# A transformer block on one core: order of VectorE's rows around the norms, short sums in last rows, and the first tiles of the second FFN in turn

## The chip, the cores and the metric

The kernel runs on one core of a Trainium2 chip. The metric is the device time of one execution in microseconds (us). The kernel before takes 1902.46 us, the median of three runs (1902.03 to 1902.89).

## The reference

One encoder block for 256 tokens of width 2048: a half-step SwiGLU FFN (inner width 5632), a mixing stage of 16 attention heads of width 128, and a second FFN. Shift, scale and gate of each come from one vector c.

```python
def rms_norm(x, g):
    y = xf * lax.rsqrt(jnp.mean(xf * xf, axis=-1, keepdims=True) + EPS)
    return (y * g.astype(jnp.float32)).astype(x.dtype)
...
mod = jax.nn.silu(c) @ w_ada[l] + b_ada[l]
sh1, sc1, gt1, sh2, sc2, gt2, sh3, sc3, gt3 = jnp.split(mod, N_MOD, axis=-1)
f = swiglu(modulate(rms_norm(h, g_ffn1[l]), sh1, sc1), w1_gate[l], w1_up[l], w1_down[l])
h = h + 0.5 * gt1[:, None, :] * f
nrm = modulate(rms_norm(h, g_mix[l]), sh2, sc2)
qkv = nrm @ w_qkv[l]
...
qa = rms_norm(q[:, :, :N_HEADS_NA], qn_na[l])
qb = partial_rope(rms_norm(q[:, :, N_HEADS_NA:], qn_dil[l]), cos, sin)
...
o_na = rms_norm(o_na.reshape(B, S, D_NA), g_out_na[l])
o_dil = rms_norm(o_dil.reshape(B, S, D_DIL), g_out_dil[l])
mix = jnp.concatenate([o_na, o_dil], axis=-1) @ w_o[l]
h = h + gt2[:, None, :] * mix
f = swiglu(modulate(rms_norm(h, g_ffn2[l]), sh3, sc3), w2_gate[l], w2_up[l], w2_down[l])
h = h + 0.5 * gt3[:, None, :] * f
```

Heads 0 to 7 attend to a neighbourhood on a grid, heads 8 to 15 to dilated windows; both kinds are computed here as full 256 x 256 scores with a bias added (-1e30 where nothing is seen).

## The kernel before

**Layout.** Activations are held transposed: h is 16 tiles of 128 features by 256 tokens, and nx holds the normed h, each tile as a rounded half (hi) beside its remainder (low). Weights come as 644 chunks of 128 x 1024, in one list (srcs) in the order of use: w1_s, a, b, d, c, e for the first FFN, w_qkv (96 chunks), w_o (32), then w2_a, b, d, c, e.

**One chunk.** SP loads it (wraw, L159, five buffers), ScalarE casts it to hi (L167), VectorE subtracts to get the remainder low (L168); hi and low have four buffers each. W.chunk asks for a chunk three ahead of the one that TensorE multiplies (AHEAD = 3). In the same place rows of w_ada are issued at a paced rate, and VectorE reduces them to the modulation vectors (L147). After a chunk that is issued with a w_ada row, that row's load is kept behind it in SP's queue.

**Products.** mm2 multiplies hi by both halves of the activation at once (512 columns, L173) and low by the first half (256 columns, L174) into a bank of 512 columns, whose two halves have to be added afterwards: by two L401 in the FFN's down product, by an ACT copy and L643 in the output projection. mm3 makes three products of 256 or 512 columns into one sum (L179), with nothing to add afterwards.

**Stages.** In the FFN the gate and up products of a tile of 128 inner features use the first k's of the model width first (up_first: 6 in the first FFN, K2 = 8 in the second), for tile after tile, then the rest; down products follow in two parts (ffn_down), whose last row d = 15 is followed by the row statistic (Stat.add) and a norm. Stat.add squares each h tile on ScalarE, or the last one on VectorE (L222), adds them up in sqa (L232), and TensorE sums over the partitions by a product with ones (pstat, L235 for sqa, L236 for the last square). rstd_from makes the reciprocal root: Ln and Exp on ScalarE (L199 is the Ln), and one Newton step on VectorE (L205, L207 to L209). norm_mod forms h times gain times root (nt, L244), adds the shift while rounding (ACT L247) and takes the remainder (L248). Around a norm TensorE runs idle matmuls (pw, L190).

**The mixing stage** is a list of units, one weight chunk each. For each of four groups of heads 8 units make v, 8 make k and 8 make q. Steps that follow are put in slots: at(u, fn) runs fn behind unit u. For k and q these are the squares (u + 1), the root over 8 values a row (u + 2, rqr) and the scaling with rope (qk_norm, u + 3, L590 to L605). The heads of a group follow 24 units later by PLAN (PLAN_L for the last group, whose heads run beside the first 16 units of the output projection): transposes of k and q (pT, L673), scores, softmax, transposes of p, and p times v. The last scores product comes with d_ew, which also adds the statistic over eight heads (ost). The projection has 32 units: b = 0 (heads 0 to 7), then b = 1, with 16 rows d each; fin scales a product (L644) by gate and root and adds it to h (L645).

**What sets the order.** TensorE's order is that of the program text (MANUAL). The order on the other engines is decided by the scheduler before the run, by priorities: a step's place in the text less an offset where it stands in tc.high_priority (URGENT = 400, SOON = 60). SP issues the loads in the order so decided, and each load waits for a free buffer.

Of the kernel before, what the change touches and what calls it, by code (L numbers as in the profile page):

```python
# [15 lines left out]
P = 128  # L16
# [35 lines left out]
PLACE = ((44, 40),) + 7 * ((48, 0),)  # L52
MANUAL = {mybir.EngineType.PE}
# [12 lines left out]
def build(tc, a):  # L66
    nc = tc.nc
    with ExitStack() as ctx:
# [47 lines left out]

        queue = []
# [93 lines left out]

        class Stat:
# [5 lines left out]
            def add(self, t, last_dve=True):  # L218
                sq = sp.tile([P, S], F32, tag="sq", name="sq")
                self.n += 1  # L220
                if self.n == self.total and last_dve:
                    nc.vector.tensor_tensor(sq, t, t, ALU.mult)  # L222
                else:
                    nc.scalar.activation(sq, t, AF.Square)
# [16 lines left out]
        def norm_mod(k, r, jsh, jsc, full=None):  # L241
            sh, gs = mods[jsh], mods[jsc]
            t = sp.tile([P, S], F32, tag="nt", name="nt")
            nc.vector.scalar_tensor_tensor(t, h[k], gs[:, k : k + 1], r, ALU.mult, ALU.mult)  # L244
            if full is not None:
                nc.scalar.activation(full, t, AF.Identity, bias=sh[:, k : k + 1])
            nc.scalar.activation(nx[k][:, 0, :], t, AF.Identity, bias=sh[:, k : k + 1])  # L247
# [53 lines left out]
        class W:  # L301
            def __init__(self):
# [5 lines left out]
                self.credit = 0.0  # L308

# [17 lines left out]
            def chunk(self, ahead=AHEAD):  # L327
                while self.head <= min(self.tail + ahead, len(srcs) - 1):
                    self.ready[self.head] = wsplit(wraw(srcs[self.head][0]), srcs[self.head][1])
# [9 lines left out]
                return self.ready.pop(self.tail - 1)  # L339

# [14 lines left out]
        def up_first(f, part, kx):  # L355
            ps = pair("pa")
            up_mm(ps, 0, kx, True, True)
            part[f] = hp.tile([P, 2, S], F32, tag="hid", name=f"pt{f}")
# [28 lines left out]
        def ffn_down(fs, hid, gate, stat=None, out=None):  # L387
            acc_ = {}
            for d, f in down_order(fs):
                if d not in acc_:  # L390
                    acc_[d] = bank("pd")
                mm2(acc_[d], *ws.next(), hid[f], f == fs[0], f == fs[-1])
# [4 lines left out]
                if d == KT - 1 and stat is not None:  # L397
                    idle(9)
                with tc.high_priority(offset=URGENT if stat is not None and d >= KT - 2 else 0):
                    for part_ in (ps[:, :S], ps[:, S:]):  # L400
                        nc.vector.scalar_tensor_tensor(h[d], part_, g, h[d], ALU.mult, ALU.add)  # L401
                    if stat is not None:
                        stat.add(h[d])
                if out is not None:
# [137 lines left out]
        with tc.tile_pool(name="att", bufs=2) as ap_, tc.tile_pool(name="atc", bufs=1) as ac:  # L542
# [71 lines left out]
            def qkv_unit(u, g, j, nm, cch, st_):  # L614
                def go(whi, wlo):
# [10 lines left out]
                    if cch == 7:  # L626
# [3 lines left out]
                        else:  # L630
                            at(u + 1, lambda: qk_squares(nm, ps, st_))
                            at(u + 2, lambda: qk_rstd(st_))
                            for t in range(2):
                                at(u + 3 + t // QS, lambda t=t: qk_norm(g, j, nm, ps, t, st_))
                return go

            def wo_unit(u, b, d):
                def fin(ps):
# [3 lines left out]
                    nc.scalar.copy(t, ps[:, :S])  # L642
                    nc.vector.tensor_tensor(t, t, ps[:, S:], ALU.add)  # L643
                    nc.vector.scalar_tensor_tensor(t, t, mods[5][:, d : d + 1], rows[b], ALU.mult, ALU.mult)  # L644
# [4 lines left out]
                def last_fin(ps):  # L649
                    if d == KT - 1:  # L650
                        idle(9)
                    with tc.high_priority(offset=URGENT):
                        fin(ps)

                def go(whi, wlo):
                    ps = bank("pso")
                    for kk in range(8):
                        sl = slice(kk * P, (kk + 1) * P)
                        mm2(ps, whi[:, sl], wlo[:, sl], ox[b * 8 + kk], kk == 0, kk == 7)
# [3 lines left out]
            def head(g, i, a0, b0, c0, d0):  # L663
                hd = g * 4 + i
                s_ = {}
# [9 lines left out]
                def a_ew():  # L675
                    with tc.high_priority(offset=SOON):
# [11 lines left out]
                def b_ew1():  # L688
                    with tc.high_priority(offset=SOON):
# [10 lines left out]
                def b_ew2():  # L700
                    with tc.high_priority(offset=SOON):
# [15 lines left out]
                def c_ew():  # L717
                    with tc.high_priority(offset=SOON):
# [11 lines left out]
                def d_ew():  # L730
                    po = s_["po"]
                    go = vec[:, GO + hd : GO + hd + 1]
                    nc.scalar.activation(ox[hd][:, 0, :], po, AF.Copy, scale=go)
                    nc.vector.scalar_tensor_tensor(
                        ox[hd][:, 1, :], po, go, ox[hd][:, 0, :].bitcast(F32), ALU.mult, ALU.subtract)
                    ost[hd // 8].add(po, False)
# [169 lines left out]
```

## Time and profile before

| | |
|---|---|
| median of three runs | 1902.46 us |
| the profiled execution, its own time | 1902.98 us |
| its span, first to last instruction | 1901.2 us |
| mean granted TensorE clock | 0.996 of full speed |
| data read from HBM | 500.09 MB, 264 GB/s over the span |
| last down product of the first FFN, start | 762.09 us |

The page gives busy times of engines: PE is TensorE's matmuls, PEld its weight loads, DVE VectorE, ACT ScalarE, POOL GpSimd, SP SyncE. A group's row reads out<-in, the tile's size, the count (x2), and in brackets how long the engine had been idle before it and what ended that: [3.02 <-DVE qn L605] is 3.02 us of idleness ended by VectorE's write of qn in line 605. A timeline row begins with the start in us and the time that its instructions took, those of a row together.

### The profile page before, as it was taken

What the parts mean: (1) busy time and instruction counts of PE and PEld (TensorE: products, weight loads), DVE (VectorE), ACT (ScalarE), POOL (GpSimd) and SP (SyncE); (2) the same over time, 40 slices, a digit from 0 to 9 for tenths busy, and PEclk for the clock granted to TensorE, in tenths of its full rate; (3) what the DMA queues carried; (4) which work ended last, traced back from release to release, by engine and by line L of the source; (5) the groups of instructions that cost most, each with busy time, mean ns of one, the idle gap of its engine ahead of it and who ended that gap; (6) DMA issues with size and microseconds to landing.
All of it is one profiled execution on the core that took longest, in us unless ns stands there. A gap on an engine that the chain in (4) does not pass through costs nothing.

```text
span 1901.2 us, 27533 instructions
## 1 busy us (share of the span) xinstructions
PE 1873.3 (99%) x10564; PEld 1633.8 (86%) x10564; DVE 1563.3 (82%) x2123; ACT 907.4 (48%) x1333; POOL 0.7 (0%) x6
## 2 busy tenths in 40 slices
PE   8999999999999999999999999999999999999999
PEld 6877888888888888888888888888888888888888
DVE  7899999988888889878887898888799986556565
ACT  2444545443334454555555565544555543334442
POOL 0000000000000000000000000000000000000000
PEclk9999999999999999999999999999999999999999
DMA  9988888889998987777765544888677876666664
GB/s 393 397 327 299 307 301 303 303 314 337 334 328 324 334 309 247 257 260 248 263 234 174 153 154 157 320 294 303 212 276 262 279 269 220 191 194 193 191 206 135
DMA packets 120227, 503.98 MB, mean 265 GB/s; under 512 B 13344, under 2 KB 15904, under 8 KB 101664
## 3 DMA queue, kind: packets, MB, share of 16 engines
q1 hardware_dynamic: 120096, 502.24, 75.9%
q8 instruction: 82, 1.34, 0.3%
q14 instruction: 49, 0.40, 0.1%
HBM read 500.09 MB, written 2.10 MB: 264 GB/s over the span
## 4 chain that ended last, share of the span: by engine, by line
PE 89%; DVE 6%; DMA 2%; ACT 1%; issue 1%; SPq 0%; ACTq 0%; DVEq 0%
PE pb L173 23%; PE pd L173 17%; PE pb L174 11%; PE pa L173 9%; PE pd L174 8%; PE pqk L179 5%; PE pqq L179 5%; PE pa L174 4%; PE pqv L179 4%; DVE low L168 2%; DMA rx<-in_w_ada_dram 2%; PE pso L173 1%; DVE rx L147 1%; DVE ra L147 1%; PE pso L174 1%
## 5 line engine op out<-in xcount | busy, mean ns | idle before, releaser
L167 ACT CAST hiw<-rw 128x1024 fp32r<-128x1024 f32 x644 | 674.6, 1050 | 713.1 <-PE pd L173 238.5
L168 DVE TENSOR_TENSOR low<-rw,hiw 128x1024 fp32r<-128x1024 f32 x644 | 785.9, 1222 | 264.3 <-ACT hiw L167 262.9
L173 PE MATMUL pb<-nx,hiw 128*128 128x512 f32 x1920 | 654.8, 389 | 0.0
L174 PE MATMUL pb<-nx,low 128*128 128x256 f32 x1920 | 530.8, 277 | 1.2 <-DVE low L168 1.2
L173 PE MATMUL pd<-hd,hiw 128*128 128x512 f32 x1408 | 480.1, 389 | 0.0
L173 PEld LDWEIGHTS pb<-nx,hiw 128*128 128x128 f32 x1920 | 360.3, 188 | 75.7
L174 PE MATMUL pd<-hd,low 128*128 128x256 f32 x1408 | 389.1, 276 | 0.0
L174 PEld LDWEIGHTS pb<-nx,low 128*128 128x128 f32 x1920 | 360.4, 188 | 1.9 <-DVE low L168 1.8
L173 PEld LDWEIGHTS pd<-hd,hiw 128*128 128x128 f32 x1408 | 264.3, 188 | 55.5
L173 PE MATMUL pa<-nx,hiw 128*128 128x512 f32 x800 | 275.1, 391 | 1.7 <-ACT hiw L167 1.2
L174 PEld LDWEIGHTS pd<-hd,low 128*128 128x128 f32 x1408 | 264.3, 188 | 0.0
L147 DVE CUSTOM_DVE_ANT_0 ra<-ra,cb,vec 128x2048 f32<-128x2048 f32 x101 | 237.0, 2346 | 3.3 <-DMA ra<-in_w_ada_dram 3.3
L174 PE MATMUL pa<-nx,low 128*128 128x256 f32 x800 | 220.9, 278 | 4.3 <-DVE low L168 4.3
L173 PEld LDWEIGHTS pa<-nx,hiw 128*128 128x128 f32 x800 | 149.5, 188 | 34.6 <-ACT hiw L167 2.4
L174 PEld LDWEIGHTS pa<-nx,low 128*128 128x128 f32 x800 | 150.2, 188 | 7.8 <-DVE low L168 6.8
L147 DVE CUSTOM_DVE_ANT_0 rx<-rx,cb,vec 128x2048 f32<-128x2048 f32 x43 | 100.9, 2347 | 1.5 <-DMA rx<-in_w_ada_dram 1.5
L173 PE MATMUL pso<-ox,hiw 128*128 128x512 f32 x256 | 90.4, 398 | 0.0
L179 PE MATMUL pqk<-hiw,nx 128*128 128x512 f32 x256 | 84.3, 395 | 0.0
L179 PE MATMUL pqq<-hiw,nx 128*128 128x512 f32 x256 | 83.0, 393 | 0.0
L179 PE MATMUL pqv<-hiw,nx 128*128 128x512 f32 x256 | 81.4, 392 | 0.3 <-ACT nx L247 0.3
L401 DVE SCALAR_TENSOR_TENSOR h<-pd,m,h 128x256 f32<-128x256 f32 x128 | 60.8, 482 | 20.0 <-PE pd L174 17.8
L174 PE MATMUL pso<-ox,low 128*128 128x256 f32 x256 | 71.6, 280 | 0.0
(138 smaller groups left out, 1510.0 us busy)
## 6 DMA issues: line engine op xcount, KB each, us to landing
ra<-in_w_ada_dram SPq DMA_DIRECT2D x101, 1024.0 KB, 7.2
rw<-in_w_b_dram SPq DMA_DIRECT2D x144, 512.0 KB, 4.5
rw<-in_w_d_dram SPq DMA_DIRECT2D x128, 512.0 KB, 4.2
rw<-in_w_a_dram SPq DMA_DIRECT2D x100, 512.0 KB, 5.2
rw<-in_w_c_dram SPq DMA_DIRECT2D x96, 512.0 KB, 4.1
rw<-in_w_qkv_dram SPq DMA_DIRECT2D x96, 512.0 KB, 4.1
rx<-in_w_ada_dram SPq DMA_DIRECT2D x43, 1024.0 KB, 7.3
rw<-in_w_e_dram SPq DMA_DIRECT2D x48, 512.0 KB, 4.5
```

The costliest lines, as they stand in the source:

```text
L147: ins = nc.vector.tensor_tensor_reduce(out=raw, in0=raw, in1=cb, scale=1.0, scalar=vec[:, BA + i : BA + i + 1], op0=ALU.mult, op1=ALU.add, ...
L167: casts[:] = casts[-1:] + [nc.scalar.copy(hi, raw)]
L168: lows[:] = lows[-1:] + [nc.vector.tensor_tensor(lo, raw, hi.bitcast(F32), ALU.subtract)]
L173: nc.tensor.matmul(out, lh, r, start=first, stop=False)
L174: nc.tensor.matmul(out[:, :S], ll, r[:, 0, :], start=False, stop=last)
L179: nc.tensor.matmul(out, l, r, start=first and i == 0, stop=last and i == 2, **kw)
L401: nc.vector.scalar_tensor_tensor(h[d], part_, g, h[d], ALU.mult, ALU.add)
```

## The change

It has six parts.

1. **rstd_first** takes the place of rstd for the two norms over h (r2 ahead of the mixing stage, r3 ahead of the second FFN). The square of the root goes to ScalarE, and the first nt is formed from the unfinished root and scaled by the Newton factor itself; norm_mod takes it as t.
2. **Late splits.** While TensorE is at the last chunk ahead of w_qkv or w2_a, the newly asked-for chunk is loaded, but its cast and remainder are put behind the statistic's last square (split_late). The chunk after it is loaded and split after the norm of k = 1 (more).
3. **Short sums.** The last row (d = 15) of both FFNs' second down part, and the last SLIM = 4 rows of the projection's b = 1, use mm3 instead of mm2: 12, 32 and 12 triples in place of pairs.
4. **Idle matmuls** ahead of a statistic: 9 become 3 (first FFN) and 5 (projection).
5. **Precedence in the mixing stage.** Squares, roots and scalings of all q and k go into high_priority SOON, URGENT for the last q. The heads of the last group get URGENT instead of SOON; d_ew gets a priority, and the statistic over eight heads (d_st) goes one unit later.
6. **up_heads** begins the second FFN: for the first KA = 3 k's four tiles take turns, then each goes on alone; w2_a is laid out to match.

```diff
+        def rstd_first(ps, n, k, jsc):
...
+            nc.scalar.activation(t0, ps, AF.Ln, scale=1.0 / n, bias=epst)
+            nc.vector.tensor_scalar(t1, ps, -0.5 / n, -0.5 * EPS, ALU.mult, ALU.add)
+            nc.scalar.activation(r, t0, AF.Exp, scale=-0.5)
+            nc.scalar.activation(t0, r, AF.Square)
+            nc.vector.scalar_tensor_tensor(t, h[k], mods[jsc][:, k : k + 1], r, ALU.mult, ALU.mult)
+            nc.vector.tensor_tensor(t0, t0, t1, ALU.mult)
+            nc.vector.scalar_tensor_tensor(t, t0, 1.5, t, ALU.add, ALU.mult)
+            nc.vector.scalar_tensor_tensor(r, t0, 1.5, r, ALU.add, ALU.mult)
+            return r, t
...
             def chunk(self, ahead=AHEAD):
+                if self.tail in (first["w_qkv"] - 1, first["w2_a"] - 1):
+                    self.late = []
                 while self.head <= min(self.tail + ahead, len(srcs) - 1):
-                    self.ready[self.head] = wsplit(wraw(srcs[self.head][0]), srcs[self.head][1])
+                    raw = wraw(srcs[self.head][0])
+                    if self.late is None:
+                        self.ready[self.head] = wsplit(raw, srcs[self.head][1])
+                    else:
+                        self.late.append((self.head, raw))
...
+            def split_late(self, ins):
+                for c, raw in self.late:
+                    self.ready[c] = wsplit(raw, srcs[c][1])
+                    after(lows[-1], ins, "late")
+                self.late = None
+
+            def more(self, ins):
+                while self.head <= self.tail + AHEAD:
+                    self.ready[self.head] = wsplit(wraw(srcs[self.head][0]), srcs[self.head][1])
+                    self.head += 1
+                    after(casts[-1], marks["act"], "late")
+                    after(lows[-1], ins, "late")
...
+        def up_heads(fs, part, kx):
+            ps = {f: pair("pa") for f in fs}
+            for k in range(KA):
+                for f in fs:
+                    for j in range(2):
+                        mm2(ps[f][:, j, :], *ws.next(), nx[k], k == 0, False)
+            for f in fs:
+                up_mm(ps[f], KA, kx, False, True)
+                park2(ps[f], f, part)
...
-                mm2(acc_[d], *ws.next(), hid[f], f == fs[0], f == fs[-1])
+                slim = d == KT - 1 and (stat is not None or out is not None)
+                if slim:
+                    wh, wl = ws.next()
+                    mm3(acc_[d][:, :S], wh, wl, hid[f][:, 0, :], hid[f][:, 1, :], f == fs[0], f == fs[-1])
+                else:
+                    mm2(acc_[d], *ws.next(), hid[f], f == fs[0], f == fs[-1])
...
-                    idle(9)
+                    idle(3)
...
-                    for part_ in (ps[:, :S], ps[:, S:]):
+                    for part_ in (ps[:, :S],) if slim else (ps[:, :S], ps[:, S:]):
...
-            r2 = st.rstd(D)
+            r2, t = rstd_first(st.ps, D, 0, 4)
             for k in range(KT):
-                last = norm_mod(k, r2, 3, 4)
+                last = norm_mod(k, r2, 3, 4, t=t if k == 0 else None)
+                if k == 1:
+                    ws.more(last)
...
+                            def soon(fn, *args):
+                                with tc.high_priority(offset=URGENT if g == 3 and j == 0 else SOON):
+                                    fn(*args)
+
+                            at(u + 1, lambda: soon(qk_squares, nm, ps, st_))
+                            at(u + 2, lambda: soon(qk_rstd, st_))
...
             def wo_unit(u, b, d):
+                slim = b == 1 and d >= KT - SLIM
...
-                        idle(9)
+                        idle(5)
                     with tc.high_priority(offset=URGENT):
                         fin(ps)
+                        if d == KT - 1:
+                            ws.split_late(hst.sq)
...
+                rank = URGENT if g == 3 else SOON
...
-                    ost[hd // 8].add(po, False)
+                def d_st():
+                    with tc.high_priority(offset=rank):
+                        ost[hd // 8].add(s_["po"], False)
...
-        for f in range(F1):
+        up_heads(range(NF1), part, K2)
+        for f in range(NF1, F1):
             up_first(f, part, K2)
```

The order of instructions follows from these priorities, so it is shown at three places, all on VectorE. The first is the end of the first FFN, from the last h to the second norm step. Before:

```order
L401 SCALAR_TENSOR_TENSOR h_82<-pd,m_90,h_82 128x256 x2
L168 TENSOR_TENSOR low<-rw,hiw 128x1024
L222 TENSOR_TENSOR sq<-h_82 128x256
L205 TENSOR_SCALAR rs_7027<-pstat 128x256
L207 TENSOR_TENSOR rs_7026<-rsr 128x256
L208 TENSOR_TENSOR rs_7026<-rs_7026,rs_7027 128x256
L209 SCALAR_TENSOR_TENSOR rsr<-rs_7026,rsr 128x256
L244 SCALAR_TENSOR_TENSOR nt<-h_79,m_92,rsr 128x256 x2
L248 SCALAR_TENSOR_TENSOR nx_97<-nt,m_91,nx_97 128x256
```

And with the change (line numbers are those of the changed file):

```order
L458 SCALAR_TENSOR_TENSOR h_82<-pd,m_90,h_82 128x256
L240 TENSOR_TENSOR sq<-h_82 128x256
L171 TENSOR_TENSOR low<-rw,hiw 128x1024
L221 TENSOR_SCALAR rs_7032<-pstat 128x256
L224 SCALAR_TENSOR_TENSOR nt<-h_79,m_92,rsr 128x256
L225 TENSOR_TENSOR rs_7031<-rs_7031,rs_7032 128x256
L226 SCALAR_TENSOR_TENSOR nt<-rs_7031,nt 128x256
L227 SCALAR_TENSOR_TENSOR rsr<-rs_7031,rsr 128x256
L263 SCALAR_TENSOR_TENSOR nt<-h_79,m_92,rsr 128x256
L267 SCALAR_TENSOR_TENSOR nx_97<-nt,m_91,nx_97 128x256
```

One h step is gone, the remainder stands behind the square, and nx_97 (the first nx) has the root's last step and the second nt ahead of it.

The second place is the last q norm (qn_10001 and qn_10007 are the same tile, the second half of the tokens), where the first units of the projection run. Before:

```order
L643 TENSOR_TENSOR wt<-wt,pso 128x256
L598 TENSOR_TENSOR ra<-qn_9962,rope 128x128
L599 TENSOR_TENSOR rb<-qn_9962,rope 128x4x16
L602 TENSOR_TENSOR rb<-qn_9962,rope 128x4x16
L644 SCALAR_TENSOR_TENSOR wt<-wt,m_93,rsr 128x256
L605 TENSOR_TENSOR qn_9962<-ra,rb 128x4x32
L645 TENSOR_TENSOR h_79<-h_79,wt 128x256
L168 TENSOR_TENSOR low<-rw,hiw 128x1024
L590 SCALAR_TENSOR_TENSOR qn_10001<-pqq_9589,rqr,gq_8601 128x128 x4
L643 TENSOR_TENSOR wt<-wt,pso 128x256
```

With the change:

```order
L651 SCALAR_TENSOR_TENSOR qn_10007<-pqq_9595,rqr,gq_8607 128x128
L666 TENSOR_TENSOR qn_9968<-ra,rb 128x4x32
L651 SCALAR_TENSOR_TENSOR qn_10007<-pqq_9595,rqr,gq_8607 128x128 x2
L211 TENSOR_TENSOR rs_9931<-rs_9931,rs_9932 128x256
L659 TENSOR_TENSOR ra<-qn_10007,rope 128x128
L660 TENSOR_TENSOR rb<-qn_10007,rope 128x4x16
L663 TENSOR_TENSOR rb<-qn_10007,rope 128x4x16
L212 SCALAR_TENSOR_TENSOR rsr<-rs_9931,rsr 128x256
L666 TENSOR_TENSOR qn_10007<-ra,rb 128x4x32
L714 TENSOR_TENSOR wt<-wt,pso 128x256 x2
L715 SCALAR_TENSOR_TENSOR wt<-wt,m_93,rsr 128x256 x2
L716 TENSOR_TENSOR h_79<-h_79,wt 128x256 x2
```

The projection's steps (wt, h) and the remainder that stood between the two halves of the norm now follow both.

The third place is the end of the projection, the last rows of h up to the statistic's last square. Before:

```order
L643 TENSOR_TENSOR wt_11037<-wt_11037,pso_10989 128x256
L232 TENSOR_TENSOR sqa_10640<-sqa_10640,sq_11011 128x256
L644 SCALAR_TENSOR_TENSOR wt_11037<-wt_11037,m5_93,rsr_10596 128x256
L645 TENSOR_TENSOR h3_82<-h3_82,wt_11037 128x256
L168 TENSOR_TENSOR low_11139<-rw_11136,hiw_11138 128x1024
L232 TENSOR_TENSOR sqa_10640<-sqa_10640,sq_11042 128x256
L643 TENSOR_TENSOR wt_11055<-wt_11055,pso_11020 128x256
L644 SCALAR_TENSOR_TENSOR wt_11055<-wt_11055,m5_93,rsr_10596 128x256
L645 TENSOR_TENSOR h3_82<-h3_82,wt_11055 128x256
L222 TENSOR_TENSOR sq_11060<-h3_82 128x256
```

With the change:

```order
L710 SCALAR_TENSOR_TENSOR wt_11034<-pso_10972,m5_93,rsr_10602 128x256
L710 SCALAR_TENSOR_TENSOR wt_11067<-pso_11009,m5_93,rsr_10602 128x256
L716 TENSOR_TENSOR h3_82<-h3_82,wt_11034 128x256
L716 TENSOR_TENSOR h3_82<-h3_82,wt_11067 128x256
L250 TENSOR_TENSOR sqa_10646<-sqa_10646,sq_11000 128x256
L250 TENSOR_TENSOR sqa_10646<-sqa_10646,sq_11037 128x256
L250 TENSOR_TENSOR sqa_10646<-sqa_10646,sq_11070 128x256
L710 SCALAR_TENSOR_TENSOR wt_11079<-pso_11042,m5_93,rsr_10602 128x256
L716 TENSOR_TENSOR h3_82<-h3_82,wt_11079 128x256
L240 TENSOR_TENSOR sq_11082<-h3_82 128x256
L171 TENSOR_TENSOR low_11088<-rw_11040,hiw_11087 128x1024
```

Ahead of the square neither L643 nor a remainder is left; the remainder stands behind it. On TensorE, pstat of the second eight heads moves behind the eight products of the first unit of b = 1.

More of the change, by code (lines that the diff above doesn't have):

```diff
@@ L52 @@
 PLACE = ((44, 40),) + 7 * ((48, 0),)
+KA = 3
+SLIM = 4
 MANUAL = {mybir.EngineType.PE}
@@ L115, in build @@
         hold = []
+        marks = {}
         queue = []
@@ L210, in rstd_from @@
             return r
+        def rstd_first(ps, n, k, jsc):
+            t0 = sp.tile([P, S], F32, tag="sq", name="rs0")
+            t1 = sp.tile([P, S], F32, tag="nt", name="rs1")
+            t = sp.tile([P, S], F32, tag="nt", name="nt")
+            r = sp.tile([P, S], F32, tag="rsr", bufs=2, name="rsr")
+            nc.scalar.activation(t0, ps, AF.Ln, scale=1.0 / n, bias=epst)
[7 more added lines that the diff above has]
+            return r, t
         class Stat:
@@ L339, in chunk @@
                 return self.ready.pop(self.tail - 1)
+            def split_late(self, ins):
+                for c, raw in self.late:
+                    self.ready[c] = wsplit(raw, srcs[c][1])
+                    after(lows[-1], ins, "late")
+                self.late = None
+            def more(self, ins):
[4 more added lines that the diff above has]
+                    after(lows[-1], ins, "late")
             def next(self):
@@ L688, in b_ew1 @@
                 def b_ew1():
-                    with tc.high_priority(offset=SOON):
+                    with tc.high_priority(offset=rank):
                         sc = ap_.tile([P, 2, S], F32, tag="sc", name="sc")
@@ L700, in b_ew2 @@
                 def b_ew2():
-                    with tc.high_priority(offset=SOON):
+                    with tc.high_priority(offset=rank):
                         sc, sm = s_["p"], s_["sm"]
@@ L717, in c_ew @@
                 def c_ew():
-                    with tc.high_priority(offset=SOON):
+                    with tc.high_priority(offset=rank):
                         s_["ph"] = ap_.tile([P, 2, S], F32R, tag="ph", name="ph")
@@ L774, in build @@
             with tc.high_priority(offset=URGENT):
-                r3 = hst.rstd(D)
+                r3, t = rstd_first(hst.ps, D, 0, 7)
                 for k in range(K2):
-                    last = norm_mod(k, r3, 6, 7)
+                    last = norm_mod(k, r3, 6, 7, t=t if k == 0 else None)
+                    if k == 1:
+                        ws.more(last)
             hold.append(last)
@@ L873, in flat @@
             return x.reshape(-1, P, P)
-        arr[f"w{l}_a"] = stream(gu[NF0 if l == 1 else 0 : F1, :, :kx])
+        if l == 1:
+            arr["w1_a"] = stream(gu[NF0:F1, :, :kx])
+        else:
+            arr["w2_a"] = stream(np.concatenate([
+                flat(gu[:NF1, :, :KA].transpose(2, 0, 1, 3, 4)), flat(gu[:NF1, :, KA:kx]),
+                flat(gu[NF1:F1, :, :kx])]))
         arr[f"w{l}_b"] = stream(np.concatenate([
```

50 lines of the change are left out of this document (31 added, 19 removed).

## Prediction

> **What bounds the kernel now.** I read the shares and the chain of waits first, then TensorE's waits, then the stretches round them.
>
> ```profile
> PE 1873.3 (99%) x10564; PEld 1633.8 (86%) x10564; DVE 1563.3 (82%) x2123; ACT 907.4 (48%) x1333; POOL 0.7 (0%) x6
> PE 89%; DVE 6%; DMA 2%; ACT 1%; issue 1%; SPq 0%; ACTq 0%; DVEq 0%
> PE pT L673 <- DVE qn L605: 3.3, 2, 3.0
> PE pstat L235 <- DVE sqa L232: 3.1, 2, 1.7
> PE pstat L236 <- DVE sq L222: 1.0, 1, 1.0
> PE pa L494 <- ACT xf L246: 4.7, 2, 4.3
> ```
>
> TensorE is the bound, and the change takes no matmul of the layer away. What it can win is time in which TensorE waits, fills with idle matmuls (pw) or runs at a low clock. A row of waits gives the total, the count and the longest. L673, L235 and L236 are waits in or at the end of the mix stage, which the change touches; L494 is the kernel's start, which it does not touch. The idle matmuls count as busy, so the two norms have to be read from the timeline (start, length).
>
> **The end of the first FFN.**
>
> ```profile
> 762.40 1.00 DVE L401 SCALAR_TENSOR_TENSOR h<-pd,m,h 128x256 f32<-128x256 f32 x2
> 763.37 1.23 DVE L168 TENSOR_TENSOR low<-rw,hiw 128x1024 fp32r<-128x1024 f32 x1
> 764.51 0.42 DVE L222 TENSOR_TENSOR sq<-h 128x256 f32<-128x256 f32 x1
> 764.98 0.70 PE L236 MATMUL pstat<-sq,ones 128*128 128x256 f32 x2
> 765.30 3.31 PEld L190 LDWEIGHTS pw<-ident,ones 128*128 128x128 f32 x28
> 765.72 0.47 ACT L199 ACTIVATE rs<-pstat,epst 128x256 f32<-128x256 f32 x1 [2.38 <-PE pstat L236]
> 766.67 0.43 DVE L207 TENSOR_TENSOR rs<-rsr 128x256 f32<-128x256 f32 x1
> 768.05 0.88 DVE L244 SCALAR_TENSOR_TENSOR nt<-h,m,rsr 128x256 f32<-128x256 f32 x2
> 769.13 0.50 PE L179 MATMUL pqv<-hiw,nx 128*128 128x512 f32 x1 [0.33 <-ACT nx L247]
> ```
>
> Before the square stand two L401 and one remainder (low). The short sum leaves one L401 (half of 1.00, so 0.5), and the remainder goes behind the square: 764.51 - 763.37 = 1.14. From the reciprocal root to nt there are three VectorE steps of 0.46 ((768.05 - 766.67) / 3) and nt itself. Now ScalarE squares while VectorE forms h times gain times root, then one product, then the scaling: one step of 0.46 less. Together 0.5 + 1.14 + 0.46 = 2.1. Two things hold some back. The 14 idle matmuls behind the second pstat end at 768.6 (765.30 + 3.31), so an earlier nx 0 would have to wait for them unless they move up with the square. And the low half of nx 0 stands behind the root's own last step and the next nt (two steps of 0.46; before, one). I take **-1.75**, between 1.2 and 2.1. The remainder put off runs while VectorE waits for pstat, 1.3 us before L207 here, so it is hidden; if the square came later it would cost up to 1.14. The next chunk's split goes into the norms, but TensorE needs that chunk only after three others at 2.7 us each. The loads that step with it on SP (a chunk before the w_ada row) have over 8 us too. Fewer idle matmuls cost nothing where TensorE would wait for the square anyway.
>
> **The last q norm.**
>
> ```profile
> 1069.53 0.16 DVE L209 SCALAR_TENSOR_TENSOR rqr<-rq,rqr 128x8 f32<-128x8 f32 x1
> 1074.87 0.27 PE L673 MATMUL pT<-ident,qn 128*128 128x128 f32 x1
> 1075.59 1.11 DVE L590 SCALAR_TENSOR_TENSOR qn<-pqq,rqr,gq 128x128 f32<-128x128 f32 x4
> 1077.82 0.28 DVE L605 TENSOR_TENSOR qn<-ra,rb 128x128 f32<-128x128 f32 x1
> 1078.16 0.40 PE L673 MATMUL pT<-ident,qn 128*128 128x128 f32 x1 [3.02 <-DVE qn L605]
> 1074.00:1078.00 4.00, 1.14 (x9) 0.82 (x7) 4.00 (x13) 1.32 (x2) 0.00 (x0) 1.00 0.25 79
> 1078.00:1082.00 4.00, 3.84 (x14) 3.31 (x15) 4.00 (x8) 0.86 (x2) 0.00 (x0) 0.57 0.44 142
> 1118.00:1124.00 6.00, 4.26 (x25) 3.63 (x25) 6.00 (x14) 3.35 (x7) 0.00 (x0) 1.00 0.33 117
> 1168.00:1172.00 4.00, 2.08 (x6) 1.53 (x7) 2.43 (x6) 0.15 (x1) 0.00 (x0) 0.80 1.02 418
> 800.00:1060.00 260.00, 259.68 (x1255) 217.18 (x1254) 208.37 (x344) 140.95 (x311) 0.00 (x0) 1.00 0.70 234
> 1060.00:1170.00 110.00, 103.50 (x624) 91.73 (x622) 101.85 (x209) 65.39 (x136) 0.00 (x0) 0.98 0.53 166
> ```
>
> The stretches give their length, then busy time of TensorE, its loads, VectorE, ScalarE and POOL, and after these the granted clock. From rqr to the last qn pass 8.6 us, of which the norm's own rows are 8 scalings of 0.27 and two ropes of some 0.7 (1077.82 + 0.28 - 1076.7, the end of the scalings, less one wt step of 0.4), together 3.6. The rest is output-projection steps and a remainder. In the new order only three steps of the row norm (0.33 each) stay between: 1069.53 + 3.6 + 1.0 = 1074.1, ahead of the transpose at 1074.87. The wait of 3.02 goes, and with it the slow clock behind it: (1 - 0.57) x 4 = 1.7. The wait of 1.7 at L235 near 1120 (the longest of its row) goes too, since pstat of the second eight heads moves behind the next output unit's 2.7 us. That is 6.4.
>
> Something is late next: VectorE. It was busy 101.85 of 110 us here. Less two remainders (2.3) and four L643 (1.6) it has 97.9 left, so this stretch cannot shrink by more than 12. Adding up its new rows by these durations, the remainders for the second unit behind the transpose and for the tenth output unit arrive 0.3 and 1.1 us after TensorE asks. I take **-5.0** (6.4 - 1.4), with 0 (all given back to remainders) and 6.4 as ends.
>
> **The end of the mix stage.**
>
> ```profile
> 1156.21 1.22 DVE L168 TENSOR_TENSOR low<-rw,hiw 128x1024 fp32r<-128x1024 f32 x1
> 1157.35 0.42 DVE L232 TENSOR_TENSOR sqa<-sqa,sq 128x256 f32<-128x256 f32 x1
> 1157.68 0.41 DVE L643 TENSOR_TENSOR wt<-wt,pso 128x256 f32<-128x256 f32 x1
> 1158.13 0.48 DVE L644 SCALAR_TENSOR_TENSOR wt<-wt,m,rsr 128x256 f32<-128x256 f32 x1
> 1158.65 0.43 DVE L645 TENSOR_TENSOR h<-h,wt 128x256 f32<-128x256 f32 x1
> 1158.99 1.22 DVE L168 TENSOR_TENSOR low<-rw,hiw 128x1024 fp32r<-128x1024 f32 x1
> 1165.29 0.28 PE L174 MATMUL pso<-ox,low 128*128 128x256 f32 x1
> 1170.59 1.22 PE L236 MATMUL pstat<-sq,ones 128*128 128x256 f32 x2 [1.01 <-DVE sq L222]
> 1171.85 0.47 ACT L199 ACTIVATE rs<-pstat,epst 128x256 f32<-128x256 f32 x1 [4.04 <-PE pstat L236]
> 1175.88 0.47 PE L173 MATMUL pa<-nx,hiw 128*128 128x512 f32 x1
> 1182.75 0.39 PE L173 MATMUL pa<-nx,hiw 128*128 128x512 f32 x1
> ```
>
> A unit of the projection costs VectorE 1158.99 - 1156.21 = 2.78, a little over TensorE's 2.72, so it ends late: the last product is done at 1165.40 (1165.29 and 0.11 for 256 columns), and pstat has its square 5.2 us later. The new order puts another row between the steps that depend on each other, where a step costs 0.33 as sqa does here instead of 0.45 and 0.52, so a unit falls to about 2.5; the four short units lose L643, and two remainders (1.14 each) go behind the square. VectorE then catches up, and what is left behind the last product is scaling, adding, square (0.52 + 0.45 + 0.45, and 0.2 for the start), 1.6 us at best; I take 2.2, so **-3.0** (0.5 to 3.6). Then from pstat to the first matmul of the second FFN: 5.3 us now, of which 0.5 comes from the slow clock (Ln starts 1.26 after pstat, 1171.85 - 1170.59; at the first norm 0.74, 765.72 - 764.98). With that and the step of 0.46, less the later low half, 4.5: **-0.8**. Then the second FFN's first 16 pairs of matmuls took 6.87 us (1182.75 - 1175.88) at 0.34 a pair, 5.44 at TensorE's own pace: one tile has only four matmul pairs for each two norms. With four tiles in turn a k has 8 pairs, 2.72 us, and norms with their remainders run ahead: **-1.3**.
>
> **The tail and the short sums.**
>
> ```profile
> 854.35 0.71 PE psc L179 x6
> 1897.05 0.23 PE pd L173
> 1897.43 1.00 DVE L401 SCALAR_TENSOR_TENSOR h<-pd,m,h 128x256 f32<-128x256 f32 x2 [3.07 <-PE pd L174]
> ```
>
> At the very end one of two L401 goes (half of 1.00): **-0.5**. The short sum is three matmuls of 256 columns, 0.71 / 2 = 0.355 for a triple, where a pair costs 0.34 (0.23 for its 512 columns, half as much for 256): 56 triples (12 + 32 + 12) by 0.015 are **+0.8**. The other, small wait of L673 goes with the earlier norms: **-0.3**. The rest of the precedence moves rows inside stretches in which TensorE does not wait; I cost it at nothing, as remainders are three chunks (8 us) ahead, and a norm with rope holds VectorE for about 5.
>
> **Sum**: 1.75 + 5.0 + 3.0 + 0.8 + 1.3 + 0.5 + 0.3 - 0.8 = 11.9 us, from the profiled execution's 1902.98 (a span of 1901.2), which lies 0.5 above the median of 1902.46. So **1890.6** against the median.
>
> **Rivals.**
> VectorE becomes the bound of the projection: the 5.0 is given back as waits for remainders. For it: 101.85 busy of 110. Against: interleaved steps are shorter. 1902.5 - 6.9 = 1895.6. Chance 0.17.
>
> The clock: with 9 idle matmuls cut to 3 and 5, TensorE could be slow at both norms. At a granted clock of 0.80, as at 1168, 3.31 us of idle matmuls would take 0.8 more (3.31 / 0.8 - 3.31), and Ln came 0.5 later there: 1.3 a norm, 2.6 in all, 1893.2. Against: the wait of 1.7 left the clock at 1.00 (1118 to 1124), and the gaps I expect are below that. Chance 0.07. [...]
>
> Slower: norms put ahead of remainders in the projections of q, k and v. From the point where VectorE falls over 6 us behind, TensorE waits for a remainder, and a wait of 3 us costs 3.02 + 1.7 = 4.7 as at 1078. Four of the seven norms moved make 19: about 1909. Against: from 800 to 1060 VectorE is busy 208.37 of 260 us, 80%, and TensorE is idle for 0.3. Chance 0.04.
>
> The change does not do what it says: an order decided beforehand, with VectorE as late as before, 1901. Chance 0.04.
>
> **Chances.** The forecast has 0.68. Its own range, from the ends of its terms, is 1887 to 1894; the first rival and the clock stretch it to 1896.5. A measurement of this kernel tells about 0.2% (3.8 us) from no change. Faster by more: 0.68 + 0.17 + 0.07, 0.92. Within: 0.05. Slower: 0.03.
>
> **What would show it.** Right: no wait of pT for qn; granted clock 1.0 at 1075 to 1090; pstat's square 2 to 3 us after the last product; no gaps in the first 16 pairs of the second FFN; one L401 at the end. Wrong: waits of pso, pqv or pqk for low; a granted clock below 0.9 behind either norm; the first matmul of the mix stage later than 5 us after the first FFN's last.

## The result, and the profile after

The changed kernel takes 1889.65 us (six runs, 1889.38 to 1891.08) against 1902.5 for the kernel before on the same chip: a ratio of 0.9934, with a 95% interval from 0.9922 to 0.9947. That is 12.85 us less. The profiled execution took 1889.59, with a span of 1887.8; before, 1902.98 and 1901.2.

The page of the kernel after, busy times and the chain that ended last:

```profile
PE 1866.0 (99%) x10600; PEld 1630.3 (86%) x10600; DVE 1556.9 (82%) x2117; ACT 905.4 (48%) x1331; POOL 0.7 (0%) x6
PE 94%; DVE 3%; DMA 2%; ACT 1%; issue 0%; SPq 0%; ACTq 0%; DVEq 0%
```

TensorE's share of the chain rises from 89 to 94%, VectorE's falls from 6 to 3%: what went is time in which TensorE waited for VectorE. TensorE's busy time falls too, by 7.3 us, although the trace counts 36 more of its rows (56 more in the short sums; ten idle matmuls fewer, which stand there as two rows each, 28 for 14). Time at half clock counts as busy (before, all 3.41 us from 1078.28 to 1081.69, at a clock of 0.50), and so do idle matmuls (before, 3.29 us from 765.52), so this is no contradiction.

TensorE's waits after (total, count, longest; the start's and the first FFN's rows left out):

```profile
PE pso L177 <- DVE low L171: 0.7, 1, 0.7
PE pa L176 <- DVE nx L267: 0.6, 1, 0.6
```

The three rows that the prediction quoted, pT for qn, pstat for sqa and pstat for sq, are gone. Two short ones are new: a product of the projection waits 0.7 for a remainder, and the first of the second FFN 0.6 for the low half of nx 0.

The first norm, from the last product of the first FFN (timeline of the kernel after: start, length):

```profile
761.51 0.28 PE L182 MATMUL pd<-hd,low 128*128 128x256 f32 x1
761.83 0.48 DVE L458 SCALAR_TENSOR_TENSOR h<-pd,m,h 128x256 f32<-128x256 f32 x1 [1.07 <-PE pd L182]
762.35 0.42 DVE L240 TENSOR_TENSOR sq<-h 128x256 f32<-128x256 f32 x1
762.69 1.22 DVE L171 TENSOR_TENSOR low<-rw,hiw 128x1024 fp32r<-128x1024 f32 x1
762.83 0.70 PE L254 MATMUL pstat<-sq,ones 128*128 128x256 f32 x2
766.45 0.50 PE L182 MATMUL pqv<-hiw,nx 128*128 128x512 f32 x1
767.16 0.30 PEld L182 LDWEIGHTS pqv<-hiw,nx 128*128 128x128 f32 x2 [0.41 <-DVE nx L267]
```

VectorE had been idle for 1.07 us when the last product came; one h step and the square follow at once, and the remainder lies under pstat. From the last product to the first of the mixing stage pass 4.94 us, 7.04 before. The last row shows what stays late: a load of weights waits 0.41 for the low half of nx 0.

The stretches behind the first norm, at the last q norm, at the end of the projection and behind the second norm (each row: length, busy time of TensorE, its loads, VectorE, ScalarE, POOL, then the granted clock):

```profile
766.00:770.00 4.00, 4.00 (x20) 2.92 (x19) 3.89 (x9) 2.98 (x6) 0.00 (x0) 1.00 0.72 281
1074.00:1082.00 8.00, 8.00 (x50) 6.96 (x49) 7.99 (x15) 3.58 (x8) 0.00 (x0) 1.00 0.54 154
1158.00:1162.00 4.00, 4.00 (x33) 3.60 (x32) 3.73 (x8) 1.31 (x3) 0.00 (x0) 1.00 0.12 14
1166.00:1170.00 4.00, 4.00 (x25) 3.53 (x24) 3.95 (x8) 1.98 (x5) 0.00 (x0) 1.00 0.81 281
```

The end of the projection in the timeline:

```profile
1158.08 0.28 PE L182 MATMUL pso<-ox,low 128*128 128x256 f32 x1
1158.39 0.48 DVE L710 SCALAR_TENSOR_TENSOR wt<-pso,m,rsr 128x256 f32<-128x256 f32 x1
1158.91 0.43 DVE L716 TENSOR_TENSOR h<-h,wt 128x256 f32<-128x256 f32 x1
1159.37 0.42 DVE L240 TENSOR_TENSOR sq<-h 128x256 f32<-128x256 f32 x1
1159.71 1.22 DVE L171 TENSOR_TENSOR low<-rw,hiw 128x1024 fp32r<-128x1024 f32 x1
1159.85 0.70 PE L254 MATMUL pstat<-sq,ones 128*128 128x256 f32 x2
1164.27 0.47 PE L176 MATMUL pa<-nx,hiw 128*128 128x512 f32 x1 [0.60 <-DVE nx L267]
```

TensorE is busy all through 1074 to 1082, with VectorE at 7.99 of 8.00, and the clock is 1.00 in all four stretches. Behind the last product VectorE has only scaling, adding and square left, and pstat follows it by 1.77 us (5.30 before).

### The profile page after: what moved, and what is told of

Its sections match the earlier page's. It is cut to its first block, busy times and chain, and to the rows that moved or that the text cites. A ratio compares the mean times of both kernels' runs of the same rounds, so it can differ in the third digit from the quotient of the medians.

```text
span 1887.8 us, 27587 instructions
## 1 busy us (share of the span) xinstructions
PE 1866.0 (99%) x10600; PEld 1630.3 (86%) x10600; DVE 1556.9 (82%) x2117; ACT 905.4 (48%) x1331; POOL 0.7 (0%) x6
## 4 chain that ended last, share of the span: by engine, by line
PE 94%; DVE 3%; DMA 2%; ACT 1%; issue 0%; SPq 0%; ACTq 0%; DVEq 0%
PE pb L176 23%; PE pd L176 17%; PE pb L177 12%; PE pa L176 9%; PE pd L177 8%; PE pqv L182 5%; PE pqk L182 5%; PE pqq L182 5%; PE pa L177 5%; PE pso L176 3%; DMA rx<-in_w_ada_dram 2%; PE pso L177 1%; DVE rx L150 1%; DVE low L171 1%; DVE ra L150 1%; PE pso L182 1%
## 5 line engine op out<-in xcount | busy, mean ns | idle before, releaser
L176 PE MATMUL pd<-hd,hiw 128*128 128x512 f32 x1384 | 471.9, 389 | 0.0
L177 PE MATMUL pd<-hd,low 128*128 128x256 f32 x1384 | 382.5, 276 | 0.0
L176 PEld LDWEIGHTS pd<-hd,hiw 128*128 128x128 f32 x1384 | 259.8, 188 | 54.5
L177 PEld LDWEIGHTS pd<-hd,low 128*128 128x128 f32 x1384 | 259.8, 188 | 0.0
L176 PE MATMUL pso<-ox,hiw 128*128 128x512 f32 x224 | 78.8, 396 | 0.0
L177 PE MATMUL pso<-ox,low 128*128 128x256 f32 x224 | 62.6, 279 | 0.7 <-DVE low L171 0.7
```

The source lines that it names most:

```text
L176: nc.tensor.matmul(out, lh, r, start=first, stop=False)
L177: nc.tensor.matmul(out[:, :S], ll, r[:, 0, :], start=False, stop=last)
```

## The experiments

Twelve kernels were run, each the changed kernel with one part undone (a), the kernel before with one part alone (b), or the changed kernel with one thing more (c). All were timed against the kernel before on the same chip. The table gives the length of seven stretches in the profiled execution of each, from the start of one of TensorE's rows to that of another, in us, and the median:

- n1: last pd of the first FFN to the first pqv; v0: first pqv to first pqk of the first group; v3: the same of the last group
- o: first to last pso; sq: last pso to the square's pstat; n2: from there to the first pa; up: first pa to first pb of the second FFN

```
                   n1    v0     v3      o     sq    n2      up   median
before           7.04 22.00  24.45 104.36   5.30  5.29  176.02  1902.5
after            4.94 22.57  23.91  99.82   1.77  4.42  174.65  1889.65
a1_norms_plain   4.94 22.52  28.13 105.74   1.77  4.43  174.58  1899.24
a2_last_q_only   4.92 22.60  28.11  99.89   1.77  4.33  174.65  1894.01
a3_stat_back     4.93 22.58  23.90 100.93   1.77  4.34  174.68  1891.02
a4_no_slim_rows  4.93 22.62  23.90  99.37   3.31  4.42  174.61  1891.32
a5_no_late       4.93 22.56  23.90  99.80   2.50  4.33  174.66  1890.49
a6_tiles_alone   4.94 22.58  23.90  99.83   1.77  4.42  177.11  1892.09
a7_root_first    5.46 22.17  23.90  99.64   1.78  4.76  174.59  1890.14
a8_idle_2        4.93 23.83  23.90  99.64   1.77  4.42  174.62  1891.72
a10_no_more      5.65 22.12  24.33  99.61   1.77  5.04  174.65  1891.07
c1_more_later    4.93 22.67  23.91  99.79   1.77  4.42  174.62  1889.82
b1_last_q_before 7.05 21.99  24.69 104.71   5.31  5.22  175.79  1903.62
b2_last_group    7.04 22.00  24.69 100.41   4.91  4.76  176.01  1898.63
```

Where an edit doesn't reach, the stretches agree within 0.2 us, so a difference of 0.3 is read as one. The medians carry more than that: the start alone (first pa) lies between 17.8 and 18.8, and the kernel before had medians of 1902.5, 1902.47, 1902.16 and 1902.01 on the four chips used. A difference of medians below 1 us says little without the stretches.

**The norms of q and k without precedence.**

```diff
-                                with tc.high_priority(offset=URGENT if g == 3 and j == 0 else SOON):
+                                with tc.high_priority(offset=0):
```

> The changed kernel, with no precedence for the norms of q and k (the heads keep theirs). If the precedence of the last q norm is what took away the wait at 1078 in the kernel before, the transposes of the last group wait about 3.0 us for qn again, the granted clock falls behind it (1.7 us), and the small wait of the third group is back: 1889.65 + 3.0 + 1.7 + 0.5 = 1894.9. Rival: the wait has gone because the other parts (statistic later, heads URGENT) free VectorE; then it is within 1 us, 1889.6 to 1890.6.

Measured 1899.24 (ratio to before 0.9984, 0.9975 to 0.9994): 9.6 us given back, about twice what the first theory said. TensorE's waits for qn:

```profile
PE pT L751 <- DVE qn L666: 6.9, 3, 3.9
```

The longest and one of 0.6 stand at the last group, 2.4 at the third. In the projection it is 5.9 (105.74 - 99.82), near the 4.7 expected. The other 4.2 stands in the third group's transposes (v3, 28.13 - 23.91), where 0.5 was expected.

**Precedence for the last q alone.**

```diff
-                                with tc.high_priority(offset=URGENT if g == 3 and j == 0 else SOON):
+                                with tc.high_priority(offset=URGENT if g == 3 and j == 0 else 0):
```

> The changed kernel with precedence for the last q norm alone (the other seven norms of q and k without). If the last one carries the gain, only the small wait of the third group near 1000 returns: 1889.65 + 0.5 = 1890.2. Rival: the earlier norms keep VectorE's backlog small and so have a share in the gain: 1891.5 to 1893, with waits of pT or of products for low in the third and last group.

Measured 1894.01, 4.4 more than the changed kernel, which is beyond both theories. The projection is as in the changed kernel (99.89); all of the loss stands in v3. A row of TensorE's timeline, and the stretch in which it stands, of this run:

```profile
1000.15 0.33 PE L751 MATMUL pT<-ident,qn 128*128 128x128 f32 x1 [2.38 <-DVE qn L666]
```

```profile
1000.00:1004.00 4.00, 3.85 (x11) 3.04 (x12) 0.86 (x3) 0.59 (x1) 0.00 (x0) 0.57 0.73 255
```

Behind the wait of 2.38 the granted clock is 0.57 (1000 to 1004), and v3 is 4.2 longer than in the changed kernel (28.11 - 23.91). In the kernel before the same wait was 0.3 (the smaller one in the row of pT, 3.3 less 3.0). The other norms' precedence thus won only 0.5 against the kernel before, but without it the rest of the change would have lost 4 us at this place. What stands in the way there is a reduction of a w_ada row; VectorE's row of it in the kernel before, and then in this run:

```profile
989.95 2.35 DVE L147 CUSTOM_DVE_ANT_0 ra<-ra,cb,vec 128x2048 f32<-128x2048 f32 x1
994.78 2.36 DVE L150 CUSTOM_DVE_ANT_0 ra<-ra,cb,vec 128x2048 f32<-128x2048 f32 x1
```

Before, it comes ahead of the norm's first scaling (993.90); here, between the scalings (the last at 994.26) and the rope of the second half (998.19). In the traces of all runs it stands late where `more` is in the kernel, and ahead of the norm where it is not (before, b1, b2, a10). That points to `more` as what the norms' precedence makes up for; a run without either was not made.

**The last q alone, in the kernel before.** The helper `soon` of the change, put into the kernel before, with URGENT for the last q and no precedence for the others.

> The kernel before, with the one edit that the last q's squares, root and scaling get URGENT. If that wait and its clock were worth 4.7 us and nothing is late in its place: 1902.5 - 4.7 = 1897.8. Rival (VectorE is the bound of the projection's first half): the work put off makes TensorE wait for remainders or for the statistic, and 3 us or more are given back: 1900.8 or above.

Measured 1903.62, no gain (ratio 1.0007, 0.9997 to 1.0016). The wait for qn is gone, but here are TensorE's waits for the sums of squares (the longest is the first pstat, 4.65), and the stretches round it:

```profile
PE pstat L235 <- DVE sqa L232: 6.0, 2, 4.7
```

```profile
1116.00:1120.00 4.00, 1.00 (x2) 0.84 (x3) 4.00 (x11) 1.03 (x3) 0.00 (x0) 0.58 0.81 248
1120.00:1124.00 4.00, 4.00 (x14) 3.38 (x13) 3.72 (x9) 0.89 (x2) 0.00 (x0) 0.56 0.18 32
```

VectorE's timeline ahead of the end of that wait:

```profile
1115.54 1.23 DVE L168 TENSOR_TENSOR low<-rw,hiw 128x1024 fp32r<-128x1024 f32 x1
1117.01 0.48 DVE L648 SCALAR_TENSOR_TENSOR wt<-wt,m,rsr 128x256 f32<-128x256 f32 x1
1117.80 0.42 DVE L649 TENSOR_TENSOR h<-h,wt 128x256 f32<-128x256 f32 x1
1118.52 0.42 DVE L232 TENSOR_TENSOR sqa<-sqa,sq 128x256 f32<-128x256 f32 x1
```

The projection's steps that were put off (wt, h) and a remainder stand between the last heads' rows, ahead of the statistic's last sum (sqa). That is the rival in which all is given back, though to the statistic and not to remainders.

**The last q and the last group's heads, in the kernel before.**

```diff
+                rank = URGENT if g == 3 else SOON
...
-                    with tc.high_priority(offset=SOON):
+                    with tc.high_priority(offset=rank):
...
+                    with tc.high_priority(offset=URGENT if g == 3 else 0):
+                        po = s_["po"]
```

> The kernel before with the last q norm URGENT and the rows of the last group's four heads URGENT too, those behind p times v and of the statistic included; the statistic stays where it was. If the 4.65 us at pstat in the run with the last q alone came from the heads' rows queueing behind the projection's on VectorE, the wait falls to that of the run with the statistic back (1.6) and the clock stays at 1.00: 1903.6 - 3.0 - 1.8 = 1898.8. Rival: VectorE as a whole is late by as much, and the wait moves on to remainders of the projection: 1902 or above.

Measured 1898.63 (0.9982, 0.9973 to 0.9991). TensorE's waits at the two statistics:

```profile
PE pstat L235 <- DVE sqa L232: 1.9, 1, 1.9
PE pstat L236 <- ACT sq L224: 1.6, 1, 1.6
```

The 1.6 is the one at the statistic over eight heads, 4.65 in the run before this; the 1.9 is at the end of the projection. As expected, the last q pays only together with the rows that follow it: o falls by 3.95 from before.

**The statistic back in its unit.**

```diff
-                              (c0, c_pe), (c0 + 1, c_ew), (d0, d_pe), (d0 + (0 if d0 == LAST else 1), d_ew), (d0 + 1, d_st)):
+                              (c0, c_pe), (c0 + 1, c_ew), (d0, d_pe), (d0 + (0 if d0 == LAST else 1), d_ew),
+                              (d0 + (0 if d0 == LAST else 1), d_st)):
```

> The changed kernel with the statistic over eight heads back in the unit of the last p times v (d_st together with d_ew), so its sums stand ahead of the first unit of b = 1 again. If the move took away the wait of 1.7 us at pstat, that wait comes back at the clock of 1.00: 1889.65 + 1.7 = 1891.4. Rival: with precedence for the heads VectorE makes the sum in time anyway: 1889.65 + 0 to 0.4.

Measured 1891.02, 1.4 more, and 1.1 in o: the wait of 1.56 is back at a clock of 1.00, less what TensorE saves elsewhere. The move is worth what the first theory said, a little less.

**The projection's last rows without short sums.**

```diff
-SLIM = 4
+SLIM = 0
```

> The changed kernel without short sums in the last four rows of the projection (SLIM = 0; the FFNs keep theirs). If the end of the projection is set by VectorE's backlog, the last rows' added step (0.45) and the backlog of three rows come back in part: pstat's square 2.6 to 3.2 us after the last product instead of 1.8, TensorE saves 32 x 0.015 = 0.5: 1889.65 + 0.3 to 0.9 = 1890.0 to 1890.5. Rival: the short sums carry most of the 3.5 us gained at this place: 1892 or above.

Measured 1891.32, 1.7 more. pstat's square comes 3.31 after the last product instead of 1.77, a little above the range expected, and o shrinks by 0.45 (expected 0.5). The spans of the profiled executions differ by 1.2 (1889.0 and 1887.8), which these two stretches account for; the rest of the 1.7 lies outside the span or is noise. So the short sums win 1.5 and cost 0.45; of the 3.5 us gained here (5.30 - 1.77) they are less than half.

**No split put off.**

```diff
-                if self.tail in (first["w_qkv"] - 1, first["w2_a"] - 1):
-                    self.late = []
...
-                for c, raw in self.late:
+                for c, raw in self.late or []:
```

> The changed kernel with no split put off: the chunk asked for last before w_qkv and before w2_a is cast and subtracted where it was, ahead of the statistic's last square. If that remainder stood in the chain, each norm is later by up to 1.14: 1889.65 + 1.1 (first norm) + 0.5 to 1.1 (second) = 1891.3 to 1891.9. Rival: VectorE has room for it before the last product ends (busy 93 to 97% here, so not much): 1889.65 to 1890.2.

Measured 1890.49, 0.8 more: 0.7 at the second norm (sq 2.50) and nothing at the first (n1 4.93). VectorE's timeline of this run at the first norm shows why:

```profile
758.80 1.00 DVE L456 SCALAR_TENSOR_TENSOR h<-pd,m,h 128x256 f32<-128x256 f32 x2
760.48 1.23 DVE L171 TENSOR_TENSOR low<-rw,hiw 128x1024 fp32r<-128x1024 f32 x1 [0.67 <-ACT hiw L170]
761.62 0.42 DVE L250 TENSOR_TENSOR sqa<-sqa,sq 128x256 f32<-128x256 f32 x1
762.29 0.48 DVE L456 SCALAR_TENSOR_TENSOR h<-pd,m,h 128x256 f32<-128x256 f32 x1 [0.25 <-PE pd L182]
762.80 0.42 DVE L240 TENSOR_TENSOR sq<-h 128x256 f32<-128x256 f32 x1
```

The remainder lies in VectorE's idle time ahead of the last row of h. The one that stood in the chain before was that of the chunk after it, which `more` holds back here too. Unlike what the section on the change says, the late split holds back the remainder alone, not the cast: in the kernel after the cast runs at 758.93, ahead of the square at 762.35.

**Without `more`.**

```diff
-                if k == 1:
-                    ws.more(last)
```

> The changed kernel without `more`: the chunk first + 3 is asked for by the first unit behind the norm again, the chunk first + 2 keeps its late split. In the first norm two remainders then stand between the last square and the first nt, where VectorE has room for one: the first nt is later by up to 1.1, and nx 2's low half comes sooner (0.4 to 0.6 back). 1889.65 + 0.5 = 1890.2 at the first norm alone, up to 1891.3 if the second norm is hit as well. Rival: `more` does nothing, and the late split had the whole gain: within 0.3 of 1889.65, with the first norm's path as in the changed kernel.

Measured 1891.07, 1.4 more. n1 is 0.7 longer and v0 0.45 shorter; n2 is 0.6 longer, so both norms are hit; v3 has 0.4 of a small wait for qn. The second remainder is in the way again, as expected.

**The old root.**

```diff
-            r2, t = rstd_first(st.ps, D, 0, 4)
+            r2, t = st.rstd(D), None
...
-                r3, t = rstd_first(hst.ps, D, 0, 7)
+                r3, t = hst.rstd(D), None
```

> The changed kernel with the old root (square on VectorE, root finished before the first nt). By one VectorE step of 0.46 in each of two norms, less what the later low half of nx gives back (0 to 0.3 each): 1889.65 + 0.3 to 0.9 = 1890.0 to 1890.6. Rival: the low half of nx, which has the root's last step and the next nt ahead of it in the new order, eats all of it: 1889.65 or below.

Measured 1890.14, 0.5 more: n1 + 0.52 and v0 - 0.40 at the first norm, n2 + 0.34 at the second. At the first norm the later low half of nx gives nearly all of it back.

**Tiles one after the other.**

```diff
-        up_heads(range(NF1), part, K2)
-        for f in range(NF1, F1):
+        for f in range(F1):
```

> The changed kernel with the second FFN's first tiles one after the other as before (w2_a laid out to match). If the norms of k = 1 to 7 set the pace of the first 16 pairs, they take 6.8 us instead of 5.5 again: 1889.65 + 1.3 = 1891.0. Rival: with the norms' remainders out of the way one tile keeps up: within 0.3.

Measured 1892.09, 2.4 more, and 2.5 in `up` (177.11 - 174.65), where 1.3 was expected. One row of TensorE's waits:

```profile
PE pa L176 <- DVE nx L267: 2.1, 4, 1.1
```

It is 1.1 longer than in the kernel before (176.02): behind the changed norm one tile alone waits up to 1.1 at once for the low half of an nx. The timelines of VectorE and TensorE at that wait:

```profile
1165.42 1.22 DVE L171 TENSOR_TENSOR low<-rw,hiw 128x1024 fp32r<-128x1024 f32 x1
1166.55 0.87 DVE L267 SCALAR_TENSOR_TENSOR nx<-nt,m,nx 128x256 fp32r<-128x256 f32 x2
1167.09 0.50 PE L176 MATMUL pa<-nx,hiw 128*128 128x512 f32 x1 [1.10 <-DVE nx L267]
```

The remainder that `more` puts behind k = 1 stands right ahead of the low half (k = 2) that ends the wait. A run with both edits was not made.

**`more` later.**

```diff
-                if k == 1:
+                if k == 3:
```

> The changed kernel with `more` behind the norm of k = 3 instead of k = 1. If its remainder, ahead of nx 2's low half, is what makes the first unit of the mixing stage 0.57 us longer than before, most of that is gained: 1889.65 - 0.4 = 1889.2, seen from the first product of v to the first of k (22.57 in the changed kernel, 22.0 before). Rival: VectorE's two steps a norm set that pace, and the remainder only moves: within 0.2 and 22.5 again.

Measured 1889.82, no difference, with v0 at 22.67. The rival holds. The sum of n1 and v0 is 27.5 to 27.8 in c1 and in every a run but a8 (28.8), against 29.0 before. This fits that VectorE's steps over the 16 norms set when the first unit ends, and that a remainder only moves within it.

**Two idle matmuls instead of 14.**

```diff
-            idle(14)
+            idle(2)
```

> The changed kernel with 2 idle matmuls instead of 14 behind each of the two row statistics (14 stay at no place). TensorE is then idle for about 3 us in each norm. If such a gap lowers the granted clock (as it was 0.57 after the gap of 3.02 in the kernel before, and 0.57 to 0.65 after 2.38 and 2.40), the first matmuls of the mixing stage and of the second FFN run at about half for some 3 to 4 us: 1889.65 + 2 x 1.7 = 1893.1. Rival: TensorE waits for VectorE and ScalarE there anyway and catches up: within 0.5.

Measured 1891.72 in the median, but from 1890.66 to 1894.64, where other runs of the changed kernel and its variants with as many executions spread by 0.3 to 1.8. TensorE's timeline and stretches of the profiled execution:

```profile
766.48 0.50 PE L182 MATMUL pqv<-hiw,nx 128*128 128x512 f32 x1 [2.48 <-ACT nx L266]
1165.38 0.47 PE L176 MATMUL pa<-nx,hiw 128*128 128x512 f32 x1 [3.28 <-DVE nx L267]
```

```profile
766.00:770.00 4.00, 3.52 (x9) 2.50 (x10) 3.89 (x8) 2.77 (x5) 0.00 (x0) 0.70 0.81 301
770.00:774.00 4.00, 4.00 (x17) 3.25 (x16) 2.84 (x7) 1.86 (x3) 0.00 (x0) 0.87 0.82 266
1166.00:1170.00 4.00, 4.00 (x25) 3.49 (x24) 3.96 (x8) 2.90 (x6) 0.00 (x0) 1.00 0.62 206
```

Behind the gap of 2.48 at the first norm the clock is 0.70 and then 0.87, where the changed kernel has 1.00 (766 to 774), and v0 grows by 1.26 (23.83 - 22.57). Behind the longer gap of 3.28 at the second it is 1.00. So the first theory holds at one norm of two. Why the longer gap cost nothing was not shown. The execution with a trace is the fastest of the four; the slowest had the lowest granted clock over its span, 0.995 against 0.997, but has no trace.

## Why the prediction was right

The forecast was 1890.6, the result 1889.65; by the profiled executions the sum was -11.9 and the spans differ by 13.4. Of the 1.5 between them 0.7 lies ahead of any edit (the second part of the first FFN's down products starts at 696.04 instead of 696.76) and is not the change's doing: in the other twelve traces that point lies anywhere between 695.95 and 696.63, in the two of the kernel before with one part at 696.53 and 696.63. The other 0.8 lies in the terms:

| term | predicted | measured |
|---|---|---|
| first FFN to the mixing stage (n1 and v0) | -1.75 | -2.10 + 0.57 = -1.53 |
| stalls in the projection (o, without the short sums' 0.45) | -5.0 | -4.54 - 0.45 = -5.0 |
| last product to the square's pstat (sq) | -3.0 | -3.53 |
| pstat to the second FFN (n2) | -0.8 | -0.87 |
| its first tiles (up) | -1.3 | -1.37 |
| tail | -0.5 | -0.58 |
| small wait for qn (v3) | -0.3 | -0.54 |
| short sums | +0.8 | 0.15 + 0.45 + 0.15 = +0.75 |

- **The last q.** Both halves of its price hold. Undone (a1), o grows by 5.9, for waits of 3.9 and 0.6 and 1.4 more, where 4.7 was said for 3.0 and its clock; that the 1.4 is the clock's is an estimate (mean granted clock of the profiled execution 0.996, in the changed kernel 0.999). What was missing is the condition: the 6.4 of this term were added up as two waits that go by two edits. They go by three. The last q alone moves the wait to the statistic (4.65, and 0.58 of the clock); the precedence of the last group's heads, which the prediction costed at nothing, takes 3 us of that away; and the moved statistic takes the last 1.1. The rival in which all is given back was right for the first edit by itself.
- **What is late next.** The two late remainders expected (0.3 and 1.1) became one, 0.66. With it the stalls should have fallen by 5.8 (6.4 - 0.66), not by 5.0. The other 0.8 is no wait of TensorE that the trace shows: eight units of b = 1 together take 22.61 us on TensorE (1116.11 to 1138.72) where they took 21.83 before (1124.54 to 1146.37). Why is open, so that the -5.0 came out as said is in part luck.
- **"I cost it at nothing"** held for the sum against the kernel before (v3 even gained 0.5), but not for the reason given. The other norms' precedence is no idle rearrangement: it keeps away 4.2 us (a2). The heads of the last group are not what would take them, since with their precedence alone (b2) the wait there is 0.57; the traces point to `more`. The slower rival priced such a place at 4.7.
- **The first norm's remainder** (1.14) goes because of `more`, not because of the late split, to which the prediction's words ("the remainder goes behind the square") leave it. Without `more` n1 is 0.7 longer (a10). The late split alone wins nothing there and 0.7 at the second norm.
- **The end of the projection** gained 0.5 more than the value taken, within its bounds. From the runs: 1.5 by the short sums, 0.7 by the late split. What remains of 3.5, some 1.3, was not taken apart; VectorE's unit there went from 2.78 to 2.56 us from one remainder to the next (1148.06 - 1127.60 over eight, the single ones uneven), where 2.5 was expected, and b2, which has neither of these two edits nor the new order of the projection's steps, stays at 4.91.

VectorE's remainders in the kernel after, the first and the last of that stretch of nine:

```profile
1127.60 1.22 DVE L171 TENSOR_TENSOR low<-rw,hiw 128x1024 fp32r<-128x1024 f32 x1
1148.06 1.23 DVE L171 TENSOR_TENSOR low<-rw,hiw 128x1024 fp32r<-128x1024 f32 x1
```

- **The clock.** The fewer idle matmuls ahead of the statistics cost nothing: 1.00 at both norms. The rival with 2.6 us did not come about.
- **The signs.** pstat's square came even sooner than the 2 to 3 us named. One sign of being wrong did show, in small: a wait of pso for low, 0.7. The first matmul of the mixing stage is 4.94 behind the last product, just below the limit of 5.
- **Sums and readings.** The bounds of the prediction's terms add up to 1888.3 and 1898.7, not to 1887 and 1894; the result lies within either. Between the last scaling and the last qn stand two steps of wt, not one; the 0.7 for a rope comes out with two. VectorE's idle 1.3 us at the first norm ends with L205 at 766.22, not with L207. None of this moves the sum.

## What to carry to other kernels

When a row gets precedence on a busy engine, ask which rows now stand behind it and who waits for those: here one edit alone moved a wait of 3 us to one of 4.65 further on, and only precedence for the whole chain up to TensorE's next sum made it a gain. Read what a wait costs from the stretch behind it too, since in a2, with a clock of 0.57 behind it, a wait of 2.4 us cost 4.2. Parts undone one by one need not add up to the gain, because some parts only repair what others would break.

## What the runs showed of the hardware

The granted clock after a gap of TensorE did not follow from the gap's length alone. Gaps of 1.74 (before), 1.91 (b2) and 3.28 us (a8, second norm) left it at 1.00. Behind gaps of 2.38 (a2), 2.48 (a8, first norm), 3.02 (before) and 4.65 (b1) the stretches of 4 us show 0.56 to 0.70. The stretch with two gaps of 1.33 and 1.01 close together in the kernel before (1168 to 1172) shows 0.80.

In the kernel before, the two stretches at a lower clock near 1078 and 1170 are these, the first behind the gap of 3.02, the second from within the gap of 1.01 on:

```profile
1078.28:1081.69 3.41, 3.41 (x12) 2.93 (x13) 3.41 (x6) 0.86 (x2) 0.00 (x0) 0.50 0.34 95
1170.44:1173.85 3.41, 3.26 (x13) 3.08 (x14) 1.50 (x5) 0.89 (x2) 0.00 (x0) 0.50 0.58 240
```

By these two rows such a stretch costs up to half of 3.41, 1.7 us (an estimate; in a2 the wait of 2.38 cost 4.2 in all). What decided between the gap of 2.48 and that of 3.28 in a8 was not shown: the two differ in length and in place, and no run varied one of these alone.
